# A decoder layer in float32r half splits: k-tiles 4 to 7 of the first x turned by VectorE and DRAM, and units of weights 3 to 5 in another room

## The chip, the cores and the metric

The kernel runs on one NeuronCore of a Trainium2 chip. The metric is the device time of one execution in microseconds (us), as a median over runs. Beside it there is one profiled execution with a trace of every instruction and every DMA.

## The reference, cut to what matters

One decoder layer on x of 256 tokens by 2048 channels, float32. The change touches only the head of its first part, the first feed-forward half:

```python
x = x + 0.5 * swiglu(rmsnorm(x, ffn1_norm), ffn1_w_gate, ffn1_w_up, ffn1_w_down)   # D_MODEL 2048, D_FF 5632
x = x + hybrid_mixer(rmsnorm(x, mix_norm), ...)     # attention and gMLP, merged by gates
x = x + 0.5 * swiglu(rmsnorm(x, ffn2_norm), ffn2_w_gate, ffn2_w_up, ffn2_w_down)
return rmsnorm(x, final_norm)

def rmsnorm(x, g):  return x * rsqrt(mean(x * x) + 1e-6) * g
def swiglu(x, w_gate, w_up, w_down):  return (silu(x @ w_gate) * (x @ w_up)) @ w_down
```

## The kernel before

Every product with a weight matrix runs on TensorE in fp32r, a shortened float32. To keep the precision each operand is split into a high part and a low part (the rest), and three matmuls are made for each tile: high by high, low weight by high x, high weight by low x (`wh,xhi`, `wl,xhi`, `wh,xlo` in the profile).

**Weights.** A gemm is a block of 512 output columns over all k-tiles (128 rows each; 16 of them for the first part). The list `hus` holds, in the order of work, half units: two k-tiles of one gemm. I call the i-th of them *step i*. One step is 12 matmuls of 128x512 (two k-tiles, two halves of 128 tokens, three products). Two steps make a *unit* of weights, 1 MB, loaded by `load_unit` (L125 to L136) on SyncE's DMA queue into one of three buffers of the tag `raw` (`RAWB = 3`). `split(i)` (L138 to L147) makes the parts of step i: ScalarE copies the high part `wh` (L146), then VectorE subtracts and writes the low part `wl` (L147). There are four buffers of `wh` and `wl`, so that split i+4 waits for the matmuls of step i.

The first four gemms are interleaved (`FIRST`): steps 0 to 7 need only the k-tiles 0 to 3 of x, steps 8 to 15 the k-tiles 4 to 7, step 16 is the first with k-tile 8, step 18 the first with k-tile 12. So unit 4 is the first whose steps (8 and 9) need k-tiles 4 and 5 of x.

**x.** x comes in with the tokens on the partitions and has to be turned, multiplied by the norm's gain (`gcols`) and split into `xhi` and `xlo`. There are two ways to turn it. `first_transposes(k)` lets TensorE transpose one k-tile into PSUM (two instructions, L248), and `first_evac(k)` reads it from there (ScalarE L252, VectorE L253). `turn_x(i, n, c, lag, read)` turns four k-tiles, the 512 channels of block c, by way of DRAM: at step i VectorE transposes blocks of 32x32 into a tile `bt` (L198) and SyncE writes it to a DRAM tile `bm` (512 KB, L182); at step i + read SyncE reads it back in another order with four DMAs of 128 KB into a tile `xt` (L188); at step i + lag ScalarE and VectorE make `xhi` (four instructions, L280) and `xlo` (eight, L282). Before the change the k-tiles 0 to 7 are turned by TensorE (k-tiles 4 to 7 in the middle of step 3), and the blocks 2 and 3 of x by DRAM, from steps 5 and 9 on.

**Order.** The order on every engine is the order in which the program emits instructions. The main loop emits, for each step i, its matmuls, then the callbacks registered `at(i, ...)` in the order of their registration, then `advance`, which loads units and splits ahead: after step 1 it goes up to split 3, after step 2 to split 5, after step 3 to split 7, and so on. Each engine takes its instructions in this order, SyncE its DMA issues: one that waits holds up all issues behind it.

Of the kernel before, what the change touches and what calls it, by code (L numbers as in the profile page):

```python
# [8 lines left out]
F32 = mybir.dt.float32  # L9
# [7 lines left out]
P = 128  # L17
S = 256
NT = S // P
D = 2048  # L20
KD = D // P
FF = 5632
NC = 512
# [13 lines left out]
RAWB = 3  # L37
UK = 4
# [3 lines left out]
def layer(ctx: ExitStack, tc: tile.TileContext, a, out):  # L42
    nc = tc.nc
    PE, ACT, DVE, POOL, SP = nc.tensor, nc.scalar, nc.vector, nc.gpsimd, nc.sync
    big = ctx.enter_context(tc.tile_pool(name="big", bufs=1))
# [8 lines left out]
    def tp_bank(name):  # L54
        return ps.tile([P, NC], F32, tag="tp", bufs=4, name=name)
# [28 lines left out]
    x = big.tile([P, NT, D], F32, name="x")  # L84
    xv = a["x"][0].rearrange("(t p) d -> p t d", p=P)

    def load_x(c0, c1):
        SP.dma_start(x[:, :, c0:c1], xv[:, :, c0:c1])
# [5 lines left out]
    gcols = sb.tile([P, 64], F32, name="gcols")  # L94
# [24 lines left out]
    def at(i, fn):  # L119
        callbacks.setdefault(i, []).append(fn)  # L120

    raws, splits = {}, {}


    def load_unit(i, parts=(0, 4)):  # L125
        if i not in raws:
            raws[i] = big.tile([P, UK, NC], F32, tag="raw", bufs=RAWB, name=f"raw{i}")
        (g, u, j), (h, v, _) = hus[2 * i], hus[2 * i + 1]
        first, last = parts
        while first < last:  # L130
            end = last if (g, u) == (h, v) or first > 1 else min(last, 2)
            q, w, k = (g, u, 0) if first < 2 else (h, v, 2)
            o = 2 * hus[2 * i + k // 2][2] - k if (g, u) != (h, v) else 0
            k0 = q["rows0"] + w * UK * P
            src = q["w"][k0:k0 + UK * P, q["c0"]:q["c0"] + NC].rearrange("(k p) c -> p k c", p=P)
            SP.dma_start(raws[i][:, first:end], src[:, first + o:end + o])  # L136
            first = end

    def split(i, k=slice(0, 2)):
        r = raws[i // 2][:, 2 * (i % 2):2 * (i % 2) + 2, :]  # L140
        if i not in splits:
            wh = big.tile([P, 2, NC], F32R, tag="wh", bufs=LA + 1, name=f"wh{i}")
            wl = big.tile([P, 2, NC], F32R, tag="wl", bufs=LA + 1, name=f"wl{i}")
            splits[i] = (wh, wl)
        wh, wl = splits[i]
        ACT.activation(wh[:, k], r[:, k], AF.Copy)  # L146
        DVE.tensor_tensor(wl[:, k], r[:, k], wh[:, k].bitcast(F32), op=OP.subtract)  # L147
# [11 lines left out]
    def products(i, ts=range(NT), jjs=range(2), high_first=False):  # L159
        g, u, j = hus[i]  # L160
        for jj in jjs:
            for group in (("hh", "lh"), ("hl",)) if high_first else (("hh", "hl", "lh"),):
                for t in ts:
                    for kind in group:
                        product(i, jj, t, kind)
        if u * UK + 2 * j + 2 == g["nk"] and ts[-1] == NT - 1 and jjs[-1] == 1:
            g["post"](i, [in_order(b) for b in g["ps"]])
# [7 lines left out]
    def turn(i, name, q, put, dst, ev, lag=8, read=3):  # L175
        got = {}

        def blocks():
            d = sb.tile([P, 4, q, 32], F32, tag="gate", bufs=2, name=f"bt{name}")
            put(d)  # L180
            m = got["m"] = dram.tile([P, 4, q * 32], F32, tag="turn", name=f"bm{name}")
            SP.dma_start(m, d.rearrange("p j m b -> p j (m b)"))  # L182

        def back():
            got["e"] = e = dst()
            m = got["m"].rearrange("(i a) j r -> j a i r", a=32)
            for j in range(4):
                SP.dma_start(e[32 * j:32 * j + 32].rearrange("p (i r) -> p i r", i=4), m[j])  # L188

        at(i, blocks)  # L190
        at(i + read, back)
        at(i + lag, lambda: ev(got["e"].rearrange("p (i m b) -> p m i b", i=4, b=32)))

    def put_tokens(src):
        def put(d):
            v = src()
            for t in range(NT):
                DVE.transpose(d.rearrange("p j (k t) b -> p t k j b", t=NT)[:, t],  # L198
                              v[:, t].rearrange("p (k j b) -> p k j b", j=4, b=32))
        return put  # L200

    def put_flat(src):
# [4 lines left out]
    def flat(v):  # L207
        return v.rearrange("p t c -> p (t c)")

    def turned(ap):  # L210
        return ap.rearrange("p k (t i b) -> p (k t) i b", t=NT, b=32)
# [24 lines left out]

    first_banks = {}

    def first_place(k):
        if k < 4:  # L240
            b = first_banks[k] = first_banks.get(k) or tp_bank(f"xt{k}")
            return b[:, 0:S]
        return first_banks[2 + k % 2][:, S:NC] if k < 6 else first_banks[2 + k % 2][:, 0:S]

    def first_transposes(k):
        b = first_place(k)
        for t in range(NT):
            PE.transpose(b[:, t * P:(t + 1) * P], x[:, t, k * P:(k + 1) * P], ident)  # L248

    def first_evac(k):  # L250
        src, g = first_place(k), gcols[:, k:k + 1]
        ACT.activation(xT["hi"][:, k], src, AF.Copy, scale=g)  # L252
        DVE.scalar_tensor_tensor(xT["lo"][:, k], src, g, xT["hi"][:, k].bitcast(F32), op0=OP.mult, op1=OP.subtract)  # L253

    def residual(e, n, c, banks, scale, norm):
        cs = slice(c * NC, (c + 1) * NC)

        def add():
            for t in range(NT):
                DVE.scalar_tensor_tensor(two(x[:, t, cs]), banks[t], scale, two(x[:, t, cs]),  # L260
                                         op0=OP.mult, op1=OP.add)
            if norm:
                if c == 0:
                    norm_open(n)
                norm_squares(n, c)

        at(e + 1, add)
        if not norm:
            return
        if c == 3:  # L270
            at(e + 2, lambda: norm_rstd(n))

        turn_x(e + (6 if c == 1 else 2), n, c, 6)

    def turn_x(i, n, c, lag, read=3):
        def evac(src):
            for k in range(4 * c, 4 * c + 4):
                v, g = src[:, 2 * (k - 4 * c):2 * (k - 4 * c) + 2], gcols[:, 16 * n + k:16 * n + k + 1]
                hi, lo = turned(xT["hi"][:, k:k + 1]), turned(xT["lo"][:, k:k + 1])
                ACT.activation(hi, v, AF.Copy, scale=g)  # L280
                for t in range(NT):
                    DVE.scalar_tensor_tensor(lo[:, t], v[:, t], g, hi[:, t].bitcast(F32),  # L282
                                             op0=OP.mult, op1=OP.subtract)

        turn(i, f"x{n}_{c}", 8, put_tokens(lambda: x[:, :, c * NC:(c + 1) * NC]),
             lambda: flat(sb.tile([P, NT, NC], F32, tag="gate", bufs=2, name=f"xt{n}_{c}")), evac, lag, read)


# [417 lines left out]
    for c in range(4):  # L706
        gemm(a["w_out"][0], c * NC, 0, KD, lambda: (mix["mhi"], mix["mlo"]),
             lambda e, banks, c=c: residual(e, 2, c, banks, 1.0, True), PAIR if c == 0 else (1, None))
# [60 lines left out]
    n = len(hus)  # L769
# [4 lines left out]


    load_unit(0, (0, 1))
    load_x(0, S)
    for k in (1, 2, 3):
        load_unit(0, (k, k + 1))
    load_x(S, NC)  # L780
    for k in (0, 1):
        load_unit(1, (k, k + 1))
    for k in (2, 3):
        load_unit(1, (k, k + 1))
    load_unit(2, (0, 2))
    load_x(NC, 2 * NC)
    load_unit(2, (2, 4))
    load_x(2 * NC, 3 * NC)
    wb = tp_bank("warm")


# [7 lines left out]
    b = tp_bank("gc0")  # L799
# [25 lines left out]
        at(8 + c, lambda c=c: norm_squares(0, c))  # L825
    at(12, lambda: norm_rstd(0))

    loaded, done = 3, 3

    def advance(to):  # L830
        nonlocal loaded, done
        while done < min(n, to):
            while loaded < n // 2 and loaded < done // 2 + RAWB:
                load_unit(loaded)
                loaded += 1
            split(done)
            done += 1

    for c, i in ((2, 5), (3, 9)):
        turn_x(i, 0, c, 5, 2)
    at(2, lambda: load_x(3 * NC, D))

    def first_x(ks):
        for k in ks:
            first_transposes(k)
        for k in ks:
            first_evac(k)
# [6 lines left out]
    for i in range(n):  # L856
        if i < n - LA - 1:
            products(i, jjs=(0,), high_first=i < 6)
            if i == 1:
                first_x((2, 3))  # L860
            if i == 3:
                first_x(range(4, 8))
            products(i, jjs=(1,), high_first=i < 6)
        for f in callbacks.pop(i, []):
            f()
        if i > 0:
            advance(i + LA + min(i - 1, 2))
# [54 lines left out]
```

## Time and profile before

| what | us |
|---|---|
| median of 3 runs | 2044.56 (2044.51 to 2045.76) |
| the profiled execution's own time | 2044.48 |
| its span, first to last instruction | 2042.8 |
| TensorE (PE) busy | 2033.4 |
| VectorE (DVE) busy | 1192.8 |
| ScalarE (ACT) busy | 966.8 |

The 1.7 us between the span and the time lie before the first and behind the last instruction. A busy PE counts matmuls that overlap: one takes 379 ns from start to end, but the next starts about 215 ns after it.

### The profile page before, as it was taken

To read this page: it belongs to the slowest core of one execution; us is meant where nothing else is said; L and a number is where in the kernel's file an instruction comes from. 1 tells how busy PE (TensorE), PEld (TensorE's weight loads), DVE (VectorE), ACT (ScalarE), POOL (GpSimd) and SP (SyncE) were. 2 spreads that over 40 slices of the span, in tenths; PEclk is the share of its full clock that TensorE was granted. 3 is DMA by queue.
4 is the path that set the end of the run, shared out by engine and by line. 5 is a ranking of instruction groups with operands and counts; after the bars stand their busy time and mean duration, and the time that the engine had idled before them with its cause. 6 is when DMAs were issued, how large, how long until landed. Compare 5 with 4: busy or idle time off the path is not lost.

```text
span 2042.8 us, 23907 instructions
## 1 busy us (share of the span) xinstructions
PE 2033.4 (100%) x9485; PEld 1780.0 (87%) x9485; DVE 1192.8 (58%) x1260; ACT 966.8 (47%) x1062; POOL 14.3 (1%) x19
## 2 busy tenths in 40 slices
PE   9999999999999999999999999999999999999998
PEld 8888888888888888888888888888888888888887
DVE  6555555455556657676665555675555555555554
ACT  6444444444444555454454444455444444444443
POOL 0000000000000000000000000000000000000000
PEclk9999999999999999999999999999999999999999
DMA  9777876676767866787866666787676666777664
GB/s 329 227 240 221 275 241 221 206 224 221 241 222 236 256 206 205 233 284 252 267 222 221 220 221 211 240 267 226 222 240 222 224 205 206 226 222 241 231 214 144
DMA packets 248633, 471.52 MB, mean 231 GB/s; under 512 B 11597, under 2 KB 40137, under 8 KB 248393
## 3 DMA queue, kind: packets, MB, share of 16 engines
q1 hardware_dynamic: 248200, 469.47, 70.9%
q8 instruction: 74, 1.21, 0.2%
q10 hardware_dynamic: 320, 0.53, 0.1%
q14 instruction: 39, 0.31, 0.0%
HBM read 440.30 MB, written 29.66 MB: 230 GB/s over the span
## 4 chain that ended last, share of the span: by engine, by line
PE 99%; issue 0%; ACT 0%; DVE 0%; POOLq 0%; POOL 0%
PE mm L156 98%; PE sp L476 0%; PE warm L796 0%; PE pv L642 0%; PE sc L605 0%; PE sc L603 0%; PE pv L638 0%; PE xt L248 0%; ACT x L758 0%; PE pv L639 0%; DVE x L743 0%; POOLq L917 0%; POOL rf L750 0%; ACT xhi L252 0%; DVE junk L745 0%
## 5 line engine op out<-in xcount | busy, mean ns | idle before, releaser
L147 DVE TENSOR_TENSOR wl<-raw,wh 128x1024 fp32r<-128x1024 f32 (+1 forms) x779 | 947.6, 1219 | 821.0 <-ACT wh L146 817.2
L146 ACT ACTIVATE wh<-raw 128x1024 fp32r<-128x1024 f32 (+1 forms) x779 | 817.5, 1053 | 1011.8 <-PE mm L156 982.6
L156 PE MATMUL mm<-wh,xhi 128*128 128x512 f32 x2144 | 813.3, 379 | 0.2 <-ACT xhi L252 0.2
L156 PE MATMUL mm<-wh,xlo 128*128 128x512 f32 x2144 | 812.7, 379 | 0.0
L156 PE MATMUL mm<-wl,xhi 128*128 128x512 f32 x2144 | 810.6, 379 | 0.0
L156 PEld LDWEIGHTS mm<-wh,xlo 128*128 128x128 f32 x2144 | 405.2, 189 | 57.8 <-DVE xlo L253 0.3
L156 PEld LDWEIGHTS mm<-wh,xhi 128*128 128x128 f32 x2144 | 405.2, 189 | 57.6 <-ACT xhi L252 0.4
L156 PEld LDWEIGHTS mm<-wl,xhi 128*128 128x128 f32 x2144 | 405.2, 189 | 57.3
L156 PE MATMUL mm<-wh,hhi 128*128 128x512 f32 x704 | 266.8, 379 | 0.0
L156 PE MATMUL mm<-wl,hhi 128*128 128x512 f32 x704 | 266.8, 379 | 0.0
L156 PE MATMUL mm<-wh,hlo 128*128 128x512 f32 x704 | 266.8, 379 | 0.0
L156 PEld LDWEIGHTS mm<-wh,hlo 128*128 128x128 f32 x704 | 133.1, 189 | 18.9
L156 PEld LDWEIGHTS mm<-wh,hhi 128*128 128x128 f32 x704 | 133.1, 189 | 18.9
L156 PEld LDWEIGHTS mm<-wl,hhi 128*128 128x128 f32 x704 | 133.1, 189 | 18.9
L156 PE MATMUL mm<-wh,uT 128*128 128x512 f32 x192 | 58.0, 379 | 0.0
L156 PE MATMUL mm<-wh,mhi 128*128 128x512 f32 x128 | 48.5, 379 | 0.0
L156 PE MATMUL mm<-wl,mhi 128*128 128x512 f32 x128 | 48.5, 379 | 0.0
L156 PE MATMUL mm<-wh,mlo 128*128 128x512 f32 x128 | 48.5, 379 | 0.0
L156 PEld LDWEIGHTS mm<-wh,uT 128*128 128x128 f32 x192 | 36.3, 189 | 5.1
L156 PE MATMUL mm<-wl,uT 128*128 128x512 f32 x96 | 36.4, 379 | 0.0
L321 DVE SCALAR_TENSOR_TENSOR sg<-mm,rstd,sg 128x512 f32<-128x512 f32 x44 | 30.9, 743 | 0.0
L226 ACT ACTIVATE junk<-x 128x512 bf16<-128x512 f32 x30 | 18.9, 628 | 25.0 <-DVE x L260 18.6
(150 smaller groups left out, 600.4 us busy)
## 6 DMA issues: line engine op xcount, KB each, us to landing
raw<-in_w_in_dram SPq DMA_DIRECT2D x92, 1024.0 KB, 5.1
raw<-in_ffn_w_down_dram SPq DMA_DIRECT2D x88, 1024.0 KB, 5.0
raw<-in_ffn_w_up_dram SPq DMA_DIRECT2D x87, 1024.0 KB, 5.2
raw<-in_ffn_w_gate_dram SPq DMA_DIRECT2D x86, 1024.0 KB, 5.1
raw<-in_w_out_dram SPq DMA_DIRECT2D x16, 1024.0 KB, 5.1
raw<-in_w_sg_out_dram SPq DMA_DIRECT2D x12, 1024.0 KB, 6.2
bmh<-bth SPq DMA_DIRECT2D x22, 512.0 KB, 2.7
sg<-bmh SPq DMA_DIRECT2D x88, 128.0 KB, 5.1
```

Of the source, the lines that this page charges most:

```text
L146: ACT.activation(wh[:, k], r[:, k], AF.Copy)
L147: DVE.tensor_tensor(wl[:, k], r[:, k], wh[:, k].bitcast(F32), op=OP.subtract)
L156: PE.matmul(g["ps"][t], act[:, k, t * P:(t + 1) * P], in_turn(w[:, jj]), start=k == 0 and kind == "hh", stop=k == g["nk"] - 1 and kind == ...
L226: ACT.activation(junk, x[:, t, c * NC:(c + 1) * NC], AF.Square, accum_out=ss[n][:, t, c:c + 1])
L321: DVE.scalar_tensor_tensor(two(sg[:, t]), banks[t], rstd[:, t:t + 1], two(sg[:, t]), op0=OP.mult, op1=OP.mult)
```

## The change

There are three edits. First, the loads at the start come in another order: x block 1 goes ahead of the last two quarters of unit 1, unit 2 follows whole, then unit 3; x block 2 and block 3 go to a callback at step 2, alternating with units 4 and 5. Second, the units 3 to 5 don't take the three `raw` buffers but one tile `more` with the tag `A`, the room in which the feed-forward values `hhi` stand later. Third, the k-tiles 4 to 7 of x (block 1) are no longer transposed by TensorE in step 3 but turned by VectorE and DRAM: blocks at step 1, read back at step 2, parts made at step 4. Between and behind the two 32x32 transposes of that turn stand the two halves of split 3, so that `advance` begins with split 4. The turn of block 2 moves from step 5 to step 6.

```diff
+    def load_unit(i, parts=(0, 4)):
+        if i not in raws and RAWB <= i < 2 * RAWB:
+            if i == RAWB:
+                raws["more"] = big.tile([P, RAWB * UK, NC], F32, tag="A", name="more")
+            raws[i] = raws["more"][:, (i - RAWB) * UK:(i - RAWB + 1) * UK]
         if i not in raws:
             raws[i] = big.tile([P, UK, NC], F32, tag="raw", bufs=RAWB, name=f"raw{i}")
...
-    def put_tokens(src):
+    def put_tokens(src, between=lambda t: None):
         def put(d):
             v = src()
             for t in range(NT):
                 DVE.transpose(d.rearrange("p j (k t) b -> p t k j b", t=NT)[:, t],
                               v[:, t].rearrange("p (k j b) -> p k j b", j=4, b=32))
+                between(t)
         return put
...
-    def first_place(k):
-        if k < 4:
-            b = first_banks[k] = first_banks.get(k) or tp_bank(f"xt{k}")
-            return b[:, 0:S]
-        return first_banks[2 + k % 2][:, S:NC] if k < 6 else first_banks[2 + k % 2][:, 0:S]
-
     def first_transposes(k):
-        b = first_place(k)
+        b = first_banks[k] = tp_bank(f"xt{k}")
...
-    def turn_x(i, n, c, lag, read=3):
+    def turn_x(i, n, c, lag, read=3, **between):
...
-        turn(i, f"x{n}_{c}", 8, put_tokens(lambda: x[:, :, c * NC:(c + 1) * NC]),
+        turn(i, f"x{n}_{c}", 8, put_tokens(lambda: x[:, :, c * NC:(c + 1) * NC], **between),
...
     load_x(S, NC)
     for k in (0, 1):
         load_unit(1, (k, k + 1))
+    load_x(NC, 2 * NC)
     for k in (2, 3):
         load_unit(1, (k, k + 1))
-    load_unit(2, (0, 2))
-    load_x(NC, 2 * NC)
-    load_unit(2, (2, 4))
-    load_x(2 * NC, 3 * NC)
+    load_unit(2)
+    load_unit(3)
...
-    loaded, done = 3, 3
+    loaded, done = 6, 4
...
-    for c, i in ((2, 5), (3, 9)):
+    turn_x(1, 0, 1, 3, 1, between=lambda t: split(3, slice(t, t + 1)))
+    for c, i in ((2, 6), (3, 9)):
         turn_x(i, 0, c, 5, 2)
-    at(2, lambda: load_x(3 * NC, D))
+
+    def more_loads():
+        load_unit(4)
+        load_x(2 * NC, 3 * NC)
+        load_unit(5)
+        load_x(3 * NC, D)
+
+    at(2, more_loads)
...
             if i == 1:
                 first_x((2, 3))
-            if i == 3:
-                first_x(range(4, 8))
```

Steps 4 and 5 still make the products with `wh` of a k-tile ahead of those with `wl` (`high_first` for i < 6); from step 6 on the order within a step is `wh,xhi`, `wl,xhi`, `wh,xlo`.

## Rows read from the trace of the kernel before

**Rows 1.** The page, busy time of each engine over the span; and all waits of PE in the whole span (engine, line, what it waited for: us in total, times, longest us).

```profile
PE 2033.4 (100%) x9485; PEld 1780.0 (87%) x9485; DVE 1192.8 (58%) x1260; ACT 966.8 (47%) x1062; POOL 14.3 (1%) x19
...
PE warm L796 <- PEq L905: 0.8, 1, 0.8
PE mm L156 <- ACT xhi L252: 0.2, 1, 0.2
```

**Rows 2.** The chain that ended last, its piece in step 3 (start, us); then PE's timeline: the first matmul of step 4, the last of step 7 and the first two of step 8 (start, us, engine, line, operation).

```profile
15.80 0.87 PE xt L248 x8
...
17.80 0.38 PE L156 MATMUL mm<-wh,xhi 128*128 128x512 f32 x1
...
27.95 0.38 PE L156 MATMUL mm<-wh,xlo 128*128 128x512 f32 x1
28.16 0.38 PE L156 MATMUL mm<-wh,xhi 128*128 128x512 f32 x1
28.38 0.38 PE L156 MATMUL mm<-wl,xhi 128*128 128x512 f32 x1
```

**Rows 3.** The timeline of SyncE's queue: start of the DMA issue, us that the issue took, what (x4 is four issues in a row).

```profile
8.79 0.37 SPq L88 DMA_DIRECT2D x<-in_x_dram  x1
9.49 0.37 SPq L136 DMA_DIRECT2D raw<-in_ffn_w_up_dram  x1
...
13.99 0.37 SPq L136 DMA_DIRECT2D raw<-in_ffn_w_gate_dram  x1
...
27.47 0.34 SPq L182 DMA_DIRECT2D bmx<-btx  x1
28.58 0.37 SPq L136 DMA_DIRECT2D raw<-in_ffn_w_up_dram  x1
30.39 1.76 SPq L188 DMA_DIRECT2D xt<-bmx  x4
...
34.51 0.34 SPq L182 DMA_DIRECT2D bmx<-btx  x1
35.89 0.38 SPq L136 DMA_DIRECT2D raw<-in_ffn_w_gate_dram  x1
41.27 1.74 SPq L188 DMA_DIRECT2D xt<-bmx  x4
43.32 3.32 SPq L136 DMA_DIRECT2D raw<-in_ffn_w_up_dram  x2
```

**Rows 4.** The timeline of ACT (start, us, operation, idle time before it and what ended it). The rows of L146 are split 3, split 4, split 5, splits 6 and 7, splits 8 and 9; those of L280 make the high parts of x blocks 2 and 3; L170 is the first write of `hhi`.

```profile
11.65 1.06 ACT L146 ACTIVATE wh<-raw 128x1024 fp32r<-128x1024 f32 x1
12.92 1.06 ACT L146 ACTIVATE wh<-raw 128x1024 fp32r<-128x1024 f32 x1 [0.21 <-DMA raw<-in_ffn_w_up_dram]
15.47 1.06 ACT L146 ACTIVATE wh<-raw 128x1024 fp32r<-128x1024 f32 x1 [1.49 <-DMA raw<-in_ffn_w_gate_dram]
...
19.35 2.00 ACT L146 ACTIVATE wh<-raw 128x1024 fp32r<-128x1024 f32 x2 [0.26 <-DMA raw<-in_ffn_w_up_dram]
23.92 2.00 ACT L146 ACTIVATE wh<-raw 128x1024 fp32r<-128x1024 f32 x2 [2.56 <-DMA raw<-in_ffn_w_gate_dram]
...
37.06 1.71 ACT L280 ACTIVATE xhi<-xt,gcols 128x256 fp32r<-128x256 f32 x4 [1.09 <-DMA xt<-bmx]
...
46.20 1.71 ACT L280 ACTIVATE xhi<-xt,gcols 128x256 fp32r<-128x256 f32 x4 [1.23 <-DMA xt<-bmx]
...
94.08 1.04 ACT L170 ACTIVATE hhi<-sg 128x1024 fp32r<-128x1024 f32 x1
```

**Rows 5.** The timeline of DVE: low parts of x k-tiles 2 and 3, a half split of one k-tile, splits 3 and 4, split 8, the two transposes of x block 2, and the low parts of x block 3.

```profile
8.50 0.69 DVE L147 TENSOR_TENSOR wl<-raw,wh 128x512 fp32r<-128x512 f32 x1 [0.63 <-ACT wh L146]
...
11.46 0.87 DVE L253 SCALAR_TENSOR_TENSOR xlo<-xt,gcols,xhi 128x256 fp32r<-128x256 f32 x2
12.74 2.50 DVE L147 TENSOR_TENSOR wl<-raw,wh 128x1024 fp32r<-128x1024 f32 x2 [0.41 <-ACT wh L146]
...
25.01 1.22 DVE L147 TENSOR_TENSOR wl<-raw,wh 128x1024 fp32r<-128x1024 f32 x1 [2.21 <-ACT wh L146]
26.15 1.30 DVE L198 STREAM_TRANSPOSE btx<-x 128x512 f32<-128x512 f32 x2
...
46.74 2.19 DVE L282 SCALAR_TENSOR_TENSOR xlo<-xt,gcols,xhi 128x128 fp32r<-128x128 f32 x8 [0.52 <-ACT xhi L280]
```

**Rows 6.** Busy time by stretch (us of the span; PE, PEld, DVE, ACT, POOL; granted clock of TensorE, mean busy share of the DMA engines, GB/s): two stretches of 2 us among the first loads, and one of 1 us in which x block 3 is read back.

```profile
12.00:14.00 2.00, 2.00 (x11) 1.76 (x10) 1.55 (x2) 1.76 (x2) 0.00 (x0) 1.00 1.05 407
16.00:18.00 2.00, 2.00 (x14) 1.84 (x12) 1.44 (x2) 1.33 (x3) 0.00 (x0) 1.00 1.05 410
...
44.00:45.00 1.00, 1.00 (x6) 0.87 (x5) 0.71 (x2) 0.96 (x1) 1.00 (x1) 1.00 1.11 225
```

**Rows 7.** Single DMA issues with their size and the us from issue to landing, in the order of their issue: the issues at 27.47, 34.51, 35.89 and 43.32 of Rows 3.

```profile
bmx<-btx SPq DMA_DIRECT2D x1, 512.0 KB, 2.9
...
bmx<-btx SPq DMA_DIRECT2D x1, 512.0 KB, 6.5
...
raw<-in_ffn_w_gate_dram SPq DMA_DIRECT2D x1, 1024.0 KB, 8.1
...
raw<-in_ffn_w_up_dram SPq DMA_DIRECT2D x1, 1024.0 KB, 6.1
```

**Rows 8.** The end of the span: the last matmul in PE's timeline, and two stretches behind it with the columns of Rows 6.

```profile
2034.02 0.38 PE L156 MATMUL mm<-wh,hlo 128*128 128x512 f32 x1
...
2036.00:2038.00 2.00, 0.00 (x0) 0.00 (x0) 1.15 (x2) 1.34 (x2) 0.55 (x1) 1.00 0.02 7
2038.00:2040.00 2.00, 0.00 (x0) 0.00 (x0) 0.00 (x0) 0.00 (x0) 0.00 (x0) 0.78 1.06 367
```

More of the change, by code (lines that the diff above doesn't have):

```diff
@@ L250, in first_evac @@
     def first_evac(k):
-        src, g = first_place(k), gcols[:, k:k + 1]
+        src, g = first_banks[k][:, 0:S], gcols[:, k:k + 1]
         ACT.activation(xT["hi"][:, k], src, AF.Copy, scale=g)
```

## The prediction

> **What bounds the kernel now.** I read the busy times first, with the waits of PE. TensorE is busy for 2033.4 of 2042.8 us and waits for other engines 1.0 us in all, the last time for the first `xhi` [rows 1]. So every us taken from PE's queue is won and every us for which PE has to wait is lost; nothing later absorbs it. Then I read the chain that ended last, at the change's place: the eight transposes of k-tiles 4 to 7 stand in it with 0.87 us [rows 2]. That is all the change can win. Third come the queues of SyncE, ACT and DVE over the first 50 us: nothing that PE needs is late, but the margins are small. Up to 26 us ACT waits again and again for weights to land (1.49 us before split 5, 2.56 us before split 8) [rows 4], while the DMA engines move 407 to 410 GB/s at a full busy share [rows 6]. Split 8 ends on DVE at 25.01 + 1.22 = 26.23, and PE first needs its `wl` at 28.38, the second matmul of step 8 [rows 2, 5]: 2.15 us to spare. The change puts a DRAM round trip ahead of this unit, and the question is whether it fits into these 2.15 us.
>
> **PE.** Eight transposes go, worth 0.87 us. Step 8 then begins at 28.16 - 0.87 = 27.29 and needs its first `wl` at 27.51 [rows 2].
>
> **The first loads.** I count in blocks of 256 KB. Before, the first half of unit 2 was the 12th block and had landed at 12.92, its second half the 16th, at 15.47, and unit 3 the 22nd, at 19.35 [rows 4]. After, unit 1 is complete with block 12, so at about 12.92 instead of before 11.65; unit 2 again ends with block 16 (15.47); unit 3 with block 20, 1.3 us ahead of 19.35 (two blocks at about 0.65 us, 0.262 MB at 407 GB/s [rows 6]), so at 18.05. x block 1 (block 10) lands ahead of 12.92.
>
> **Splits 3 to 7.** After the low parts of k-tiles 2 and 3, at 12.33, DVE has transpose 0.65, half split 0.69, transpose 0.65, half split 0.69 [rows 5], ending at about 15.0 instead of 13.99 (half of the 2.50 for splits 3 and 4). PE wants the last of it in the second k-tile of step 3. Step 3 begins 2.59 (a quarter of 28.16 - 17.80) ahead of step 4, at 17.80 - 0.87 - 2.59 = 14.34; its second k-tile's `wl` is wanted 10 matmuls of 0.215 later, at 16.5: 1.5 us of cover. Split 4 (data at about 14.2, `wl` at 16.6) is wanted at 17.8, split 5 (`wl` at 17.9) at 20.4, splits 6 and 7 come earlier than before. These edits cost nothing; what hides them is that cover, and without it the 1.3 us of transposes would be paid on PE.
>
> **The turn of block 1.** Its blocks are ready at 12.33 + 0.65 + 0.69 + 0.65 = 14.3, and SyncE issues the write `bmx` at about 14.4. It is queued behind units 2 and 3. By the count of blocks it is the 22nd, and the 22nd landed at 19.35 [rows 4]. Bounds: the write at 27.47, behind little, took 2.9 us, that at 34.51, behind a unit and a read-back, 6.5 [rows 7]: 17.3 to 20.9. I take 19.35, since it follows from the bytes ahead.
>
> SyncE's next instruction is the read-back, and it waits for this landing, as at 30.39 and 41.27 [rows 3]. Queued behind it on SyncE stand the loads of unit 4, x block 2, unit 5 and x block 3 (the callback of step 2 comes after it). Before, unit 4 was issued at 13.99, when a buffer was free; now the free room is of no use to it, as it stays behind the read-back until 19.35. The DMA engines run dry meanwhile: their last bytes are those of `bmx`.
>
> From the first of the four read issues to ACT's first high part it took 46.20 - 41.27 = 4.93 with little ahead in the queue, 37.06 - 30.39 = 6.67 behind a unit [rows 3, 4]. I take 4.93: the parts of k-tiles 4 to 7 begin at 24.3 and end on DVE 46.74 + 2.19 - 46.20 = 2.73 later [rows 4, 5], at 27.0. That is before 27.3, by a hair, so it costs nothing by itself, and ACT is free for split 8 at 26.0.
>
> Unit 4 is issued behind the four reads, 43.32 - 41.27 = 2.05 after the first [rows 3], at 21.4. The unit at 43.32, in the same place behind four reads, landed 6.1 us after its issue [rows 7]; the reads move 225 GB/s, little over half of what units do [rows 6]. So unit 4 lands at 27.5, where it landed at 23.92 before. Split 8 took 26.23 - 23.92 = 2.31 from landing to the end of `wl` [rows 4, 5]: 29.8. PE wants it at 27.51. **Stall: 2.3 us**, in two pieces: about 1.3 us for `wh` ahead of the first matmul of step 8 and 1.0 for `wl` ahead of the second.
>
> A rule of the Trainium skill gives another landing. The page "DMA: Bandwidth & Descriptors", section "Anatomy of one DMA — SWDGE (gpsimd) path", has a fit for single DMAs: 2.0 us fixed and the bytes at 436 GB/s. By it `bmx` would take an estimated 3.2 us from its issue and unit 4 4.4; the trace agrees for the write at 27.47 (2.9) and not for that at 34.51 (6.5) or the unit at 43.32 (6.1) [rows 7], which queue. The sum by the fit would be 14.4 + 3.2 + 2.05 + 4.4 + 2.31 = 26.4, no stall, an estimate of 0.87 us won.
>
> **What is late next.** Unit 5 comes 1.5 MB (six blocks, 3.9 us) behind unit 4, at 31.4; split 10 ends at about 33.7 and step 10 asks for it at 29.8 + 5.2 = 35.0. Unit 6 follows 3.9 us later again (x block 3, 1 MB), while two steps give 5.2: each margin grows. The transposes of x block 2 wait on DVE behind split 9 (31.0), and the block lands at 28.8. Unit 6 no longer waits for the splits of unit 3, since it takes the buffer of unit 0. `hhi`, which shares the room, is first written at 94.08 [rows 4], some 60 us after the last split of unit 5. None of it costs.
>
> **Sum.** 2044.48 (span 2042.8 and 1.7 around it) - 0.87 + 2.3 = 2045.9; the median stands 0.08 above the profiled run, so 2046.0.
>
> **Rivals.** Differences under 0.2% (4.1 us) can't be told from no change in a measurement of this kernel; I call "same" what lies within it.
>
> *A, the forecast*: one stall of 1 to 4 us at step 8: 2044.7 to 2047.7. For it: the row of block 22 and two measured read-backs. Chance 0.52.
>
> *B, the turn stays hidden*: `bmx` passes faster than the bytes ahead suggest, landing 17.3 as at 27.47. Then unit 4's split ends at 17.3 + 2.05 + 6.1 + 2.31 = 27.8, a stall of 0.3; with a landing that is no slower than ACT's need, none. 2043.6 to 2044.7. Against it: units 2 and 3 are still coming in when it is issued (block 20 lands at 18.05). Chance 0.28.
>
> *C, the round trip is longer, and it ends slower*: the write takes the 6.5 us of the one at 34.51 and unit 4 the 8.1 of the one at 35.89 [rows 7]. Then split 8 ends at 14.4 + 6.5 + 2.05 + 8.1 + 2.31 = 33.4, PE stalls 5.9 us, net 2044.56 + 5.0 = 2049.6. It decides from a stall of 5.0 us, that is unit 4 landing after 30.2. For it: both rows come from the same turn, one with three transfers in line. Against it: behind the write nothing is in the queue this time. Chance 0.14.
>
> *D, the clock falls too*: after PE's last matmul at 2034.02 the granted clock was still full up to 2038 and 0.78 on average in the next 2 us [rows 8], so an idle time of under 3.6 us left it at 2.4 GHz. The forecast's two pieces lie below; a stall like C's could bring 1.2 GHz. At half clock each step takes 2.59 us more, so two steps on top of A's 2.3 give 2045.9 + 5.2 = 2051. Chance 0.05.
>
> *E, something outside the head moves*: chance 0.01, either sign, since nothing else in the program's order changes but SyncE's counting.
>
> **How the numbers follow.** The likeliest is A, 2046.0. Slower by over 0.2%: C's half beyond 4.1 us (0.08; its other half is stalls of 4 to 5 us), D, and half of E: 0.13. Faster by over 0.2% would take 4.1 us where PE has 0.87 to give: 0.01. Same: 0.86. The range holds A and B whole and C up to its price: 2043.4 (2044.56 - 0.87, and 0.3 for the spread of runs) to 2049.6. It leaves out D, C beyond its price, and E: about 0.15.
>
> **What would show it.** Right, if after the change: no transpose in step 3 and step 4 at about 16.9; `bmx` issued at about 14.4, the four reads from 19.35, unit 4 issued at 21.4 with DMA traffic near nothing for some 2 us in between; split 8 on ACT at about 27.5 after a wait for unit 4; PE idle twice at step 8, 2.3 us in all, before a matmul with `wh` and one with `wl`; no other wait of PE, and a full granted clock. Wrong in the term of `bmx`, if the reads start before 18 or after 21; wrong in that of unit 4, if it lands other than 6 us after its issue; wrong in the mechanism, if unit 4 is issued ahead of the reads, if PE waits for `xhi` or `xlo` of k-tile 4 instead, or if it waits in steps 3 to 7.

## The result, and the profile after

The changed kernel takes 2049.88 us (median of 17 runs, 2047.05 to 2051.32), the kernel before in the runs beside it 2044.72 (17 runs, 2044.51 to 2046.89). The medians stand 5.2 us apart, where 1.4 were forecast. The ratio, estimated from all runs, is 1.0022 (some 4.5 us), with a 95% interval of 1.0015 to 1.0028. The profiled execution took 2050.69, with a span of 2048.9. Four of the 17 runs stay under 2047.8, so the loss told below, of this one execution, is not the same in every run; no profile of a lower run is on record.

First the busy time and the four largest waits of PE in the span (two more are of 0.2 us), which answer to [rows 1]:

```profile
PE 2035.2 (99%) x9477; PEld 1780.1 (87%) x9477; DVE 1194.2 (58%) x1267; ACT 966.3 (47%) x1063; POOL 13.3 (1%) x19
...
PE mm L161 <- ACT wh L151: 2.4, 2, 1.8
PE mm L161 <- DVE wl L152: 1.6, 2, 0.8
PE warm L795 <- PEq L910: 0.8, 1, 0.8
PE xt L248 <- DMA x<-in_x_dram: 0.3, 1, 0.3
```

Eight matmul records fewer, as the edit says, and new waits: two for `wh` and two for `wl`. There is not one place where PE waits but two. PE's timeline at both of them (start, us, operation, idle time before it):

```profile
27.46 0.38 PE L161 MATMUL mm<-wh,xlo 128*128 128x512 f32 x1
28.39 0.48 PE L161 MATMUL mm<-wh,xhi 128*128 128x512 f32 x1 [0.55 <-ACT wh L151]
29.64 0.48 PE L161 MATMUL mm<-wl,xhi 128*128 128x512 f32 x1 [0.78 <-DVE wl L152]
29.96 0.38 PE L161 MATMUL mm<-wh,xlo 128*128 128x512 f32 x1
...
55.22 0.38 PE L161 MATMUL mm<-wh,xlo 128*128 128x512 f32 x1
57.41 0.48 PE L161 MATMUL mm<-wh,xhi 128*128 128x512 f32 x1 [1.81 <-ACT wh L151]
58.67 0.67 PE L161 MATMUL mm<-wl,xhi 128*128 128x512 f32 x1 [0.78 <-DVE wl L152]
...
62.40 0.38 PE L161 MATMUL mm<-wl,xhi 128*128 128x512 f32 x1
```

The first place is step 8, the forecast one. Its first three matmuls start at 28.39, 29.64 and 29.96, where without a wait each would start 0.215 after the one before: 1.85 us lost. The second is step 18, the first that needs x block 3: 3.02 us lost up to 58.67 (57.41 instead of 55.44, then 58.67 instead of 57.63). After it the nine matmuls up to 62.40 take 3.73 us instead of 1.94. The granted clock says why (columns as in [rows 6]: the granted clock is the third from the end, GB/s the last):

```profile
18.00:20.00 2.00, 2.00 (x11) 1.76 (x10) 0.61 (x2) 1.61 (x2) 0.00 (x0) 1.00 0.15 49
48.00:50.00 2.00, 2.00 (x11) 1.76 (x10) 1.28 (x2) 1.63 (x2) 0.00 (x0) 1.00 0.21 76
...
58.00:59.00 1.00, 0.33 (x1) 0.33 (x2) 1.00 (x2) 1.00 (x2) 0.00 (x0) 0.92 0.19 72
59.00:60.00 1.00, 1.00 (x4) 0.73 (x4) 1.00 (x2) 1.00 (x2) 0.00 (x0) 0.50 0.00 0
```

It is 0.50, that is 1.2 GHz, from about 58.8 on, and full again in the stretch of 62.40; 1.79 us are lost to it. In this execution step 0 also began at 6.10 instead of 5.72, as PE waited for the first x and the gains to land, whose loads no edit touches. The sum is - 0.87 + 0.38 + 1.85 + 3.02 + 1.79 = 6.17; the last matmul starts at 2040.20 instead of 2034.02 [rows 8], 6.18 later. These terms are the whole difference, to 0.01 us.

The first two rows above are stretches in which the DMA engines move 49 and 76 GB/s. In the kernel before they moved 412 and 378:

```profile
18.00:20.00 2.00, 2.00 (x11) 1.74 (x10) 1.45 (x4) 1.52 (x3) 0.00 (x0) 1.00 1.07 412
48.00:50.00 2.00, 2.00 (x11) 1.74 (x10) 2.00 (x5) 1.76 (x2) 0.00 (x0) 1.00 1.01 378
```

SyncE's queue shows what held them, and answers to [rows 3]:

```profile
14.53 0.34 SPq L187 DMA_DIRECT2D bmx<-btx  x1
19.59 1.76 SPq L193 DMA_DIRECT2D xt<-bmx  x4
21.39 0.43 SPq L141 DMA_DIRECT2D more<-in_ffn_w_gate_dram  x1
...
38.40 0.44 SPq L141 DMA_DIRECT2D raw<-in_ffn_w_gate_dram  x1
38.96 0.43 SPq L187 DMA_DIRECT2D bmx<-btx  x1
40.06 0.38 SPq L141 DMA_DIRECT2D raw<-in_ffn_w_gate_dram  x1
48.90 1.74 SPq L193 DMA_DIRECT2D xt<-bmx  x4
```

The write of block 1 is issued at 14.53 and has landed at 19.59; from then on the reads and unit 4 go out. The write of block 3 is issued at 38.96 between units 8 and 9 and has landed only at 48.90, 9.9 us later; its reads follow then. ACT waits at the end of both chains [rows 4]:

```profile
24.13 1.71 ACT L280 ACTIVATE xhi<-xt,gcols 128x256 fp32r<-128x256 f32 x4 [3.73 <-DMA xt<-bmx]
27.27 2.00 ACT L151 ACTIVATE wh<-more 128x1024 fp32r<-128x1024 f32 x2 [1.44 <-DMA more<-in_ffn_w_gate_dram]
...
54.71 1.70 ACT L280 ACTIVATE xhi<-xt,gcols 128x256 fp32r<-128x256 f32 x4 [5.08 <-DMA xt<-bmx]
56.32 3.88 ACT L151 ACTIVATE wh<-raw 128x1024 fp32r<-128x1024 f32 x4
```

At 27.27 it is unit 4 that ends the wait. At 54.71 it is block 3; before, its parts began at 46.20. Splits 18 to 21 stand behind them on ACT and run at 56.32, and it is split 18's `wh` and then its `wl` for which PE waits in step 18. The chain of work that ended last, followed back from there, leads through the high and low parts of block 3 and its reads to its write:

```profile
38.96 9.81 DMA bmx<-btx
...
57.44 1.19 DVE wl L152
```

### The profile page after: what moved, and what is told of

Read it like the earlier page. It is cut to its first block, busy times and chain, and to the rows that moved or that the text cites. A ratio compares the mean times of both kernels' runs of the same rounds, so it can differ in the third digit from the quotient of the medians.

```text
span 2048.9 us, 23903 instructions
## 1 busy us (share of the span) xinstructions
PE 2035.2 (99%) x9477; PEld 1780.1 (87%) x9477; DVE 1194.2 (58%) x1267; ACT 966.3 (47%) x1063; POOL 13.3 (1%) x19
## 4 chain that ended last, share of the span: by engine, by line
PE 96%; DMA 2%; DVE 0%; SPq 0%; issue 0%; ACT 0%; POOLq 0%; POOL 0%; ACTq 0%
PE mm L161 96%; DMA raw<-in_ffn_w_gate_dram 1%; DMA bmx<-btx 1%; DMA xt<-bmx 0%; PE sp L476 0%; PE pv L642 0%; PE sc L605 0%; PE sc L603 0%; SPq L193 0%; SPq L141 0%; DVE wl L152 0%; DVE btx L203 0%; ACT wh L151 0%; SPq L88 0%; DVE xlo L282 0%
## 5 line engine op out<-in xcount | busy, mean ns | idle before, releaser
L321 DVE SCALAR_TENSOR_TENSOR sg<-mm,rstd,sg 128x512 f32<-128x512 f32 x44 | 30.9, 743 | 0.0
```

Of the source, the lines that this page charges most:

```text
L321: DVE.scalar_tensor_tensor(two(sg[:, t]), banks[t], rstd[:, t:t + 1], two(sg[:, t]), op0=OP.mult, op1=OP.mult)
```

## The experiments

The theory was that both waits come from the DMA queue around the DRAM turns. Rival 1 was that the new load order or the shared room costs by itself; rival 2 that the second wait is only the first one handed on; a later rival that bandwidth, not the hold on SyncE, is short. Ratios are against the kernel before, run on the same chip beside them, with 95% intervals of some 0.09% (1.8 us) to either side. The kernel before itself had medians of 2044.72 to 2045.48 in the four series, and single runs up to 2047.5.

**Without the turn of block 1.** The changed kernel, with k-tiles 4 to 7 transposed by TensorE again:

```diff
-    turn_x(1, 0, 1, 3, 1, between=lambda t: split(3, slice(t, t + 1)))
...
+            if i == 3:
+                first_x(range(4, 8))
```

> The changed kernel without its third edit: k-tiles 4 to 7 go through TensorE in step 3 again, the load order and the room for units 3 to 5 stay. Theory (both stalls come from the order of SyncE's queue around the DRAM turns): no wait of PE at step 8, since nothing holds unit 4 back, and none at step 18 or well under 1 us; time 2044.3 to 2045.3, level with before. Rival 1 (the load order or the shared room costs by itself): PE still waits in steps 3 to 10 for wh or wl; 2046 or more.

2044.91 us, ratio 1.0000 (0.9991 to 1.0009), and PE waits nowhere between the first `xhi` and the end. In the stretch in which the changed kernel moved 49 GB/s this one moves 408:

```profile
18.00:20.00 2.00, 2.00 (x11) 1.74 (x10) 1.69 (x5) 1.54 (x3) 0.00 (x0) 1.00 1.05 408
```

Rival 1 falls: order and room cost nothing that this interval or this trace shows. The loss comes with the turn.

**Unit 4 ahead of the read-back.**

```diff
+    at(2, lambda: load_unit(4))
     turn_x(1, 0, 1, 3, 1, between=lambda t: split(3, slice(t, t + 1)))
...
     def more_loads():
-        load_unit(4)
```

> The changed kernel with the load of unit 4 issued at step 2 ahead of the read-back of x block 1, not behind it; nothing else moved. Theory: unit 4 is issued at about 15 and lands at about 22 to 23 instead of 27.2; what is late then is the split behind the parts of block 1 on ACT and DVE, so the 1.75 us at step 8 shrink to 0.3 to 1.0. The stall at step 18 shrinks with everything coming some 2 to 3 us earlier, but 0.5 to 2 us of it stay, since the write of block 3 still stands behind unit 8; the clock stays full; 2045 to 2047. Rival 2 (the second stall is only the first one handed on): none at step 18; 2044 to 2045. Rival 1: step 8 as before, 2049 or more.

2046.00 us, ratio 1.0005 (0.9996 to 1.0014), runs from 2044.58 to 2049.75. The profiled execution is the fastest of them: PE waits 0.5 us, once, for the `wl` of step 8, and not at step 18. The wait at step 8 shrank as expected. At step 18 this profile goes with rival 2, which wanted no wait there; the median goes with the theory. That the runs reach up to 2049.75 says that another wait comes and goes; which, this one profile can't tell.

**The write of block 3 ahead of unit 8.**

```diff
-    for c, i in ((2, 6), (3, 9)):
-        turn_x(i, 0, c, 5, 2)
+    turn_x(6, 0, 2, 5, 2)
+    turn_x(8, 0, 3, 6, 3)
```

> The changed kernel with the write of x block 3 one step earlier (step 8), so that SyncE issues it ahead of unit 8 and not behind it; the read-back stays at step 11, the parts at step 14. Theory: the stall at step 8 stays (1.5 to 2 us); the write lands some 2.6 us (1 MB) earlier than the 9.8 us after its issue, the parts begin at about 52 instead of 54.7 and the 3.0 us at step 18 shrink to under 0.8, with no fall of the clock; 2045.2 to 2046.5. Rival 2 (the second stall is the first handed on): step 18 waits 2 us or more, 2048 or more.

2048.06 us, ratio 1.0016 (1.0007 to 1.0024): 1.6 us above the range expected. The write had landed 4.4 us after its issue (38.40, reads from 42.78 on) instead of 9.9, but block 3's parts began at 52.84, only 1.9 earlier than in the changed kernel. In the profiled execution (2047.36 us) the wait at step 18 did shrink as expected, to 0.67 us with the clock full, and at step 8 PE waited 1.07 and 0.78 us. So part of the loss at step 18 went; why the median is no lower, this one profile can't tell.

**Both, and the parts of block 1 behind split 8.** The two diffs above, and

```diff
-    turn_x(1, 0, 1, 3, 1, between=lambda t: split(3, slice(t, t + 1)))
+    turn_x(1, 0, 1, 4, 1, between=lambda t: split(3, slice(t, t + 1)))
```

> Both edits (unit 4 ahead of the read-back, block 3's write ahead of unit 8), and the parts of block 1 are made at step 5 instead of 4, so behind split 8 and ahead of split 9. Theory: no wait of PE at steps 8 and 18; what is left of the change is its 0.87 us; 2043.4 to 2044.2, faster than both kernels. Rival 2 would say the same of step 18. Rival 1: 2046 or more. If the parts of block 1 are late instead, PE waits at step 8 for xhi or xlo.

2048.73 us, ratio 1.0015 (1.0006 to 1.0024), runs from 2044.56 to 2050.84. The expectation was wrong by 5 us, and this was the most useful run. Its profiled execution (2050.84 us) in rows: ACT at block 3's parts, the landing of the four reads of block 3 (issued from 41.71 on), and PE at step 18:

```profile
53.95 1.71 ACT L280 ACTIVATE xhi<-xt,gcols 128x256 fp32r<-128x256 f32 x4 [5.33 <-DMA xt<-bmx]
...
xt<-bmx SPq DMA_DIRECT2D x4, 128.0 KB, 10.3
...
56.65 0.48 PE L161 MATMUL mm<-wh,xhi 128*128 128x512 f32 x1 [2.44 <-ACT wh L151]
57.91 0.79 PE L161 MATMUL mm<-wl,xhi 128*128 128x512 f32 x1 [0.78 <-DVE wl L152]
```

At step 8 PE doesn't wait at all, and still it waits at step 18. So rival 2 falls: the second wait stands by itself. It even grew, from 3.02 to 3.64 us lost: block 3's parts come 0.8 us earlier than in the changed kernel, but PE, no longer held up at step 8, asks for step 18 at 54.06 instead of 55.44. And the theory falls in its detail. The write of block 3 is quick when it goes ahead of units 8 and 9 (issued at 37.29, landed by 41.71), but now its reads stand behind these 2 MB and land 10.3 us after their issue. In the profile of the second experiment, with unit 4 first and the write left behind unit 8, block 3's parts began at 49.99, 4 us earlier than here; that was the fastest of its runs and this is the slowest, so how much of the 4 us the order makes is not shown. My reading is that, whichever of the two goes behind the units, block 3 comes after all that the queue has to move up to then. A third turn has put 1 MB more into this queue, half of it as reads at little over half the rate [rows 6], with gaps while SyncE waits.

**Block 3 needed later.** If that is so, the order of the DMAs is the wrong handle, and the step that needs block 3 the right one. The first four gemms interleave also over k-tiles 8 to 15, and the parts of block 3 move behind split 22:

```diff
-    FIRST = (4, lambda p, q, m: 4 if q >= 4 else 3 if q >= 2 else 2 if p == 3 else q)
+    FIRST = (4, lambda p, q, m: 5 if q >= 6 else 4 if q >= 4 else 3 if q >= 2 else 2 if p == 3 else q)
...
-    for c, i in ((2, 6), (3, 9)):
-        turn_x(i, 0, c, 5, 2)
+    turn_x(6, 0, 2, 5, 2)
+    turn_x(9, 0, 3, 9, 2)
```

> The changed kernel with block 3 of x needed later: the four first gemms also interleave their k-tiles 8 to 11 and 12 to 15 (steps 16 to 23 and 24 to 31), so that k-tile 12 is first needed at step 24 instead of 18, and the parts of block 3 are made at step 18 instead of 14, behind split 22; DMA order and everything up to step 15 unchanged. Theory (step 18 waits because the DMA queue, filled and held up by three turns, brings block 3 too late, and the splits behind its parts wait with it): the 1.4 to 2 us at step 8 stay, step 18 waits for nothing, the clock stays full; 2045.2 to 2046.5 and a smaller spread than the changed kernel. Rival (it is the weights of units 8 and 9 themselves that are late, whatever block 3 does): PE still waits for wh between steps 16 and 20; 2048 or more.

2045.70 us, ratio 1.0002 (0.9994 to 1.0011), runs from 2045.14 to 2047.00. All waits of PE behind step 0 are these, both at step 8:

```profile
PE mm L161 <- ACT wh L151: 1.1, 1, 1.1
...
PE mm L161 <- DVE wl L152: 0.8, 1, 0.8
```

DMA traffic from 48 to 50 us is as thin as in the changed kernel (54 GB/s), and PE waits for none of it. The weights of units 8 and 9 were not late by themselves. The changed kernel's 2049.88, measured in another series, is 4.2 us more, or 4.9 if each is taken against the kernel before beside it; that is what step 18 and the clock behind it cost, and the profile above gave 4.8 for the two.

**The turn of block 1 on ScalarE's DMA queue.**

```diff
-    turn_x(1, 0, 1, 3, 1, between=lambda t: split(3, slice(t, t + 1)))
+    turn_x(1, 0, 1, 4, 2, queue=ACT, between=lambda t: split(3, slice(t, t + 1)))
```

(`turn` issues its write and its four reads on `queue`.)

> The changed kernel with the write and the four reads of block 1's turn issued by ScalarE on its own DMA queue, the reads at step 3 (ahead of splits 6 and 7) and the parts at step 5 (behind split 8); SyncE holds nothing for this turn and issues unit 4, x block 2, unit 5 and x block 3 at about 15. Theory (unit 4 is late because it stands behind a waiting instruction): no wait at step 8; the DMA engines don't run dry between 18 and 21 us; the write lands at about 17 to 18 since it isn't behind units 2 and 3. Step 18 is near the edge: 0 to 1.5 us; 2043.6 to 2045.5. Rival (bandwidth, not the hold: the turn's 1 MB shares the engines with the units, so something is late wherever it is issued): PE waits at steps 6 to 10, 2046 or more.

2049.88 us, ratio 1.0023 (1.0014 to 1.0032), in the rival's range and not the theory's. ACT and PE of its profiled execution:

```profile
14.45 0.35 ACTq L187 DMA_DIRECT2D bmx<-btx  x1
14.90 2.01 ACT L151 ACTIVATE wh<-raw 128x1024 fp32r<-128x1024 f32 x2 [1.22 <-DVE btx L203]
20.47 2.66 ACTq L193 DMA_DIRECT2D xt<-bmx  x4
23.23 2.95 ACT L151 ACTIVATE wh<-more 128x1024 fp32r<-128x1024 f32 x3 [6.32 <-issue]
30.91 1.72 ACT L280 ACTIVATE xhi<-xt,gcols 128x256 fp32r<-128x256 f32 x4 [4.72 <-DMA xt<-bmx]
...
24.34 0.80 PE L161 MATMUL mm<-wh,xhi 128*128 128x512 f32 x1 [2.31 <-ACT wh L151]
```

I had the write land at 17 to 18, out of the way of units 2 and 3. It landed at 20.47, 6.0 us after its issue, later than on SyncE's queue (19.59), and the reads took until 30.9: the units that SyncE could now issue kept the same DMA engines full (405 GB/s from 20 to 22 us). The Trainium skill says so on the page "DMA: Bandwidth & Descriptors", section "Issuing engines are not separate DMA queues": DMAs of several issuing engines interleave on the same 16 engines, and only issue time is saved. The rows agree. What's more, the waiting instruction now stood on ACT, and splits 6 and 7 behind it: PE waited at step 6, and the clock was 0.52 on average from 24 to 26 us. Half of the theory came true: the DMA engines did not run dry (412 GB/s from 18 to 20 us), and PE did not wait at step 8. So this run doesn't decide between the hold and the bandwidth: what came too late stood, as before, behind an instruction that waited, now on ACT, and the write that it waited for took 1.0 us longer than on SyncE's queue.

**The same with block 3 needed later**, both diffs:

> Both: block 1's turn on ScalarE's queue and block 3 needed at step 24. Theory: PE waits nowhere; only the 0.87 us of the eight transposes are left of the change: 2043.5 to 2044.2, with little spread. Rival (bandwidth): 2045 or more, with waits between steps 6 and 10.

2048.71 us, ratio 1.0015 (1.0006 to 1.0024): the wait at step 6 (2.2 and 0.8 us) and the fall of the clock stay, as the rival had it.

**Unit 4 ahead of the read-back, the parts of block 1 at step 5, block 3 needed later:**

> Unit 4 issued ahead of block 1's read-back on SyncE's queue, block 1's parts at step 5, and block 3 needed at step 24. Theory: as the one on ScalarE's queue, 2043.5 to 2044.4; step 8 has little to spare, since the parts of block 1 are ready at about 27.5 and PE wants them at 27.3 to 27.9, so up to 0.5 us may be lost there. Rival (weights late by themselves): 2046 or more.

2044.06 us (2043.65 to 2044.88), ratio 0.9991 (0.9983 to 1.0000). PE waits nowhere, apart from 0.8 us ahead of its first instruction. Split 8 on ACT and, behind it, the parts of block 1:

```profile
22.53 1.06 ACT L151 ACTIVATE wh<-more 128x1024 fp32r<-128x1024 f32 x1 [2.28 <-DMA more<-in_ffn_w_gate_dram]
24.53 1.71 ACT L280 ACTIVATE xhi<-xt,gcols 128x256 fp32r<-128x256 f32 x4 [0.94 <-DMA xt<-bmx]
```

The unit has landed at 22.5 instead of 27.3.

**Three in one series**, to see what the 0.87 us are and whether the order of split 8 and the parts matters. The kernel before with only the later block 3; the combined version again; and the combined version with the parts at step 4, ahead of split 8.

> The kernel before with only the interleaving that needs block 3 of x at step 24 (its parts at step 18): no turn of block 1, no shared room. Theory: PE waits nowhere before and nowhere here, so this edit alone gives nothing: level with the kernel before, within 0.5 us. Rival (the interleaving itself is what makes the combined version faster): 0.5 us or more below before.

> The version with unit 4 ahead of the read-back, block 1's parts at step 5 and block 3 at step 24, once more beside the two others of this call: 0.6 to 1.0 us below the kernel before and below the kernel before with block 3 later, the 0.87 us of the eight transposes; no wait of PE.

> The same with block 1's parts at step 4 again, so ahead of split 8 on ScalarE and VectorE. Theory (the parts have to wait for the read-back until about 24.5, and split 8, whose weights have long landed, waits behind them): PE waits 0.4 to 0.8 us for wl at step 8, so 0.4 to 0.8 us above the version with the parts at step 5. Rival (the order of the two makes no difference, since both are needed at step 8): level with it, within 0.2 us.

2044.80 us, 2044.30 and 2045.27; ratios 1.0000 (0.9991 to 1.0009), 0.9994 (0.9986 to 1.0003) and 1.0003 (0.9994 to 1.0012). The interleaving alone gives nothing that these runs show. The profiled execution of that run is its slowest, 2047.09 us, and has a wait that neither the expectation nor the prediction knew:

```profile
PE mm L156 <- DVE wl L147: 0.9, 2, 0.7
```

Both pieces lie between 873 and 880 us, in the mixer's products, the larger one where the low parts of a split stand on VectorE behind the turning of `k`. ACT's rows of that part come 0.50 us later than before's at 842 us and 2.69 later at 948: 2.2 us are lost between. Block 1 is not turned by DRAM in this kernel, so the wait is none of the change's. It comes and goes: the profile of before doesn't have it, that with both edits and late parts has 0.7 us of it, and the combined version's second profile 0.3, so "no wait of PE" was wrong by that. It may be what spreads the runs of the kernel before, some 3 us up from its fastest; no profile of such a run is on record.

The combined version stands 0.5 us below it by medians and 0.9 below the kernel before beside them (2045.18), where 0.6 to 1.0 was expected of both. With the parts at step 4 PE waits once more, at step 8:

```profile
28.94 0.48 PE L161 MATMUL mm<-wl,xhi 128*128 128x512 f32 x1 [0.78 <-DVE wl L152]
```

That is 0.97 us by medians above the parts at step 5, some more than the 0.4 to 0.8 expected. The combined version has the lowest median in both of its series, but the intervals (upper ends 1.0000 and 1.0003) don't put it clear of the kernel before.

## Why the prediction was right or wrong

**What bounds the kernel**: right. Every us by which PE waited reached the end, to 0.01 us in the sum above. That PE waits nowhere behind step 0 holds for the profiled execution of before, one of its fastest; other runs of this program wait in the mixer as well.

**The 0.87 us of the transposes**: right by the rows (step 3 has none). In the first profile of the combined version step 0 begins 0.29 us later than before (6.01 for 5.72), and ACT's write of `k` at 945 us comes 0.58 earlier (944.67 for 945.25): 0.87 won between the two. The medians are 1.4 and 0.9 us below those of before in the same series (2044.06 against 2045.48, 2044.30 against 2045.18); the first is more than the transposes can give, and the spread of before is in it.

**Splits 3 to 7 at no cost**: right; no wait in steps 1 to 7.

**The first stall**: right in its place and its mechanism, and near in size. The write landed at 19.6 for 19.35, unit 4 was issued at 21.39 for 21.4, landed at 27.3 for 27.5, and PE lost 1.85 us for 2.3, in the two pieces named. The start of step 0 took 0.38 of the difference. Undoing the order (unit 4 first, parts at step 5) took the stall away in all three profiles that have it.

**What is late next**: this is the step that failed. I followed the units, where each margin does grow, and x block 2, but not the write and the read-back of block 3, and said "None of it costs". It cost 3.0 us at step 18. The rows for it lay open: before, block 3's parts began at 46.20, with 1.23 us of waiting [rows 4], and with its write 6.5 us under way [rows 7]; 1 MB more in a full queue and a start of the turns some 4 us later had to be carried through to the step that needs the block. I stopped at the first late instruction. Why block 3 comes later in some runs than in others stays open.

**The clock**: I took from [rows 8] that an idle time of under 3.6 us leaves it full, and gave its fall 0.05. At step 18 PE was idle for 1.81 and 0.78 us with one matmul between, and the clock fell at about 58.8. At step 8, with 0.55 and 0.78, it didn't. Both idle times together are less than the one of [rows 8], so that row was no bound. The experiments add that one piece can do: with the turn on ScalarE's queue the clock was at 0.50 from 24.20 us on, ahead of the matmul at 24.34 that ended 2.31 us of idle time. With block 3 needed later, pieces of 1.10 and 0.78 left it full. What decides was not tried further.

**The sum**: 2046.0 was short by the two terms left out, 3.0 and 1.8 in the profiled execution. The range's upper end, 2049.6, came from rival C, a longer round trip of block 1, which did not happen. The measured median, 2049.88, lies 0.3 above that end; the ratio 1.0022 on the 2044.56 before gives 2049.1, inside it. Either way its nearness is luck of two other terms. I gave 0.86 to no change beyond 0.2%; the measured 0.22% lies just outside, and its interval reaches from 0.15 to 0.28.

## What to carry to other kernels

A round trip through DRAM on a queue that also loads weights cost this kernel more than its own time: it held the issues behind it, left the DMA engines nearly dry while the write landed (49 and 76 GB/s), and pushed back the later round trips by some 4 us. So follow such a delay to the last step that needs a turned block. Try giving what is ready the right of way, the next load ahead of the read-back and its split ahead of the parts (the latter was worth 1.0 us by medians here). And where a block is late whatever the order of the transfers, move the step that needs it rather than the transfers; that brought 4 to 5 us here, while the gain over the kernel before stayed within the noise.

## What the runs showed of the hardware that I had not expected

The granted clock fell to 1.2 GHz after two idle pieces of about 1.8 and 0.8 us with one matmul between them, and the nine matmuls that followed took 1.8 us longer; in another run it fell within one idle time of 2.31 us, although behind the last matmul of the kernel before it had stayed full for over 3.6 [rows 8]. A write of 512 KB issued on another engine's queue took 6.0 us beside loads that filled the DMA engines, more than the 5.1 from its issue to the first read on SyncE's queue. And four reads of 128 KB took 10.3 us to land behind 2 MB of weights, where they took 3.5 with little ahead of them.
